# Ranks, weight differences and first-token sums in the FFN of a decoder layer: a change of order

## The chip, the cores and the metric

One core of one Trainium2 chip runs the whole kernel. The metric is the device time of one execution, in microseconds (us); smaller is better. Figures below come from three timed runs and from one execution that the hardware profiler recorded.

## What is computed

The reference is one decoder layer on x of 512 tokens by 2048, in float32: an RMSNorm, one input projection, three token mixers side by side, an output projection with residual, and then the part that the change is about:

```
x = x + concat(ya, yb, yc) @ w_out          # 2048 x 2048
h = rmsnorm(x, ffn_norm)
x = x + (silu(h @ w_gate) * (h @ w_up)) @ w_down   # 2048 x 5632, twice; 5632 x 2048
out = rmsnorm(x, final_norm)
```

## The kernel before

**Numbers in two halves.** Every float32 operand of a product is split into a high part (`hi`, rounded by ScalarE's copy, L197) and the low rest (`lo`, VectorE's subtraction, L198). A product is then three matmuls (hi by hi, hi by lo, lo by hi). `split` (L196) does this for weights and activations alike.

**Phase 1** (attention and most of the output projection, to L1096) isn't touched, but for the name of a context manager. **Phase 2** (L1106 on) does the rest: the last 512 rows of the output projection (`pp`, then `bt` token tile by token tile in `by_token_tile`, L1143), the norm of each token tile (`tail_norm`, L1182), the FFN, and the final norm.

**The FFN products.** `w_gate` and `w_up` are worked off in chunks of 256 columns: 11 blocks of 512 columns (b), four chunks each (i = 0 to 3: gate, up, gate, up), 44 chunks. A chunk is a 2 x 2 block product (weights a, b, c, d of 128 columns by 1024 rows; activations A11, A12, A22 and the sums S1 to S4) done with seven products P1 to P7 in place of eight. Each product is 16 matmuls into one of three PSUM banks, named X (P1, P4, P6, P7), Z (P5, P3) and V (P2) with g for gate and u for up: Zg is the Z bank of a gate chunk. Weights of P5, P6, P7 and P4 are differences of the loaded blocks, made on VectorE by `sub` (L1254, its instruction at L1258). In regular chunks (42 of 44), P1's block of code makes t3 = c-b and b-a, P5's makes c-(b-a) over c, P6's makes t4 = d-c; t3 and t4 live in tiles of the tag `xq` (four tiles, L1257). The first gate and the first up chunk run interleaved and make every difference in place (`weights_in_place`, L1267); they are unchanged in this.

**Beside each chunk** runs a quarter of the down product of the block before (`down`, L1366): four steps `d` with 12 matmuls each (tile `fd`), which read `w_down` and the finished activations `aT`. It loads its running sum from DRAM (Y) into two `xq` tiles, adds `fd` to it (L1385) and stores it again (L1389). `ORDER` (L1412) is the order of a chunk: P1, d, P5, d, P6, P2, d, P7, d, P4, d, P3 (the last d only stores). When the last product of a half chunk is added, `done` runs: the gate's sum and Silu (L1345, L1346), or the up's sum (L1352), the product with the gate (L1354) and the split into `aT`.

**The hand-over.** `tail_norm` forms for the token tiles 2 and 3 the sums that the seven products need: s3 (L1194), S1 (L1195), S2 (L1196), S4 (L1197). `turn` (L1205) transposes one source on TensorE, eight 128 x 128 transposes (tile `hps`), four to a bank, through three PSUM banks (`psat`), and splits them (L1219, L1220). The list at L1401 gives the order of products and turns of the first two chunks.

**Tiles that are handed round.** Six raw tiles take all weight loads (`raws`), four `ring` tiles the high halves of chunk weights and both halves of `w_down` (`rings`), four `lo` tiles the chunks' low halves; a new user waits until the last reader of the tile is done.

**What sets the order of instructions.** TensorE's order is that of the program (L116). For the other engines and the DMA queue of SyncE a planner lays down one fixed order when the program is built: with its own estimates of durations it gives each free engine, of the instructions that are ready by then, the one of lowest rank. A rank is a running count over the program. Inside `with tc.high_priority():` the count starts again at 0, and behind the block it goes on from where it stood; so the first instruction of every such block has rank 0, its tenth rank 9, wherever the block stands. Nearly all work of phase 2 on the other engines stands in such blocks: loads and splits of weights, sums, evacuations, `tail_norm`. On the chip each engine works through its fixed order.

```
raw = raws.tile([P, 1024], F32, name=f"raw{uid[0]}", tag="raw")    # six
w = rings.tile([P, 2, 512], F32R, name=f"w{uid[0]}", tag="ring")   # four
lo = fp.tile([P, 1024], F32R, name=f"lo{uid[0]}", tag="lo", bufs=4)
```

Of the kernel before, what the change touches and what calls it, by code (L numbers as in the profile page):

```python
# [31 lines left out]
F32 = mybir.dt.float32  # L32
# [75 lines left out]
def tile_hymba(ctx: ExitStack, tc: tile.TileContext, x, attn_norm, w_in, q1, k1, q2, k2, da_norm, hg_norm,  # L108
# [46 lines left out]
    uid = [0]  # L155

# [83 lines left out]
    def wstream(src, kts, col0, n, keep=None, parts=1, step=0):  # L240
# [5 lines left out]
        for g in range(0, len(kts), per_dma):  # L246
            ks = kts[g:g + per_dma]
            uid[0] += 1
            with tc.high_priority():
# [7 lines left out]
            for a in range(0, len(ks), per):  # L257
                kk = ks[a:a + per]
                uid[0] += 1
                with tc.high_priority():  # L260
# [8 lines left out]
    def proj_d(src, col0, n, act_t, evac, name, kts=range(KT), banks=None):  # L269
# [12 lines left out]
        for j in range(n // P):  # L282
            with tc.high_priority():
                evac(j, ps[j])
# [8 lines left out]
    def proj_t(src, col0, n, act_t, evac, name, kts=range(KT), banks=None, of=None, **parts):  # L293
# [12 lines left out]
        for tt in range(NT):  # L306
            with tc.high_priority():
# [12 lines left out]
    def proj_t256(src, col0, act_t, evac, name):  # L320
# [7 lines left out]
        for j in range(2):  # L328
            with tc.high_priority():
# [6 lines left out]
    with ExitStack() as p1:  # L336
# [133 lines left out]
        def b_project(th):  # L470
# [3 lines left out]
            if th == 0:  # L474
                for j in range(2):
                    with tc.high_priority():
# [629 lines left out]
    with ExitStack() as p2:  # L1106
        fp = p2.enter_context(tc.tile_pool(name="fp", bufs=1))
# [35 lines left out]
        def by_token_tile(ccs, ws, act_of, X, tail, between=None):  # L1143

            for tt in range(NT):
                c = slice(tt * P, (tt + 1) * P)
                for i, cc in enumerate(ccs):
# [6 lines left out]
                    with tc.high_priority():  # L1154
                        ev_add(cc, X, True)(tt, ps)
                with tc.high_priority():
# [25 lines left out]
        def tail_norm(tt):  # L1182
# [8 lines left out]
            if tt >= 2:  # L1191
# [4 lines left out]
                dve.tensor_tensor(h0a, h2a, h0a, op=ALU.subtract)  # L1196
                dve.tensor_tensor(h0b, h0b, h0a, op=ALU.subtract)  # L1197
# [7 lines left out]
        def turn(k, pr):  # L1205

            src = source(k, pr)
            for b in range(2):
# [5 lines left out]
                with tc.high_priority():  # L1214
# [7 lines left out]
        for cc in range(2):  # L1222
            proj_t(w_out2, cc * 512, 512, mT, ev_add(cc, X, True), f"pp{cc}", kts=range(4), banks=banks(f"pp{cc}"))
        ws = resident(w_out2, 0, (2, 3), [fp.tile([P, 4, 2, T], F32R, name=f"wo{cc}", tag="wo", bufs=2) for cc in (2, 3)])
        early = {(2, 4): ("A11", 0), (2, 6): ("A12", 0), (3, 4): ("A11", 1), (3, 6): ("A12", 1)}
        by_token_tile((2, 3), ws, lambda k: (hi_of(mT, k), lo_of(mT, k)), X, tail_norm,
                      lambda tt, n: turn(*early[tt, n]) if (tt, n) in early else None)

        wg, wu, wd = w_gate[0], w_up[0], w_down[0]
        NB = D_FF // 512  # L1230
        A["S2"], A["S3"] = wide("S2"), wide("S3")
        C = [[slots.tile([P, 2, 512], F32, name=f"C{i}{j}", tag="slot") for j in range(2)] for i in range(2)]
        aTs = [slots.tile([P, 2, T], F32R, name=f"aT{j}", tag="slot") for j in range(4)]
        A["S4"] = [slots.tile([P, 2, 2, 256], F32R, name=f"S4{j}", tag="slot") for j in range(4)]
        XF = []

        class Chunk:


            def __init__(self, w, col, name, C, done, in_place=False):  # L1240
                self.in_place = in_place
                self.w, self.col, self.name, self.C, self.done = w, col, name, C, done
                self.raw, self.bank, self.left = {}, {}, [{"P1", "P2", "P4"}, {"P3", "P5", "P6", "P7"}]
# [16 lines left out]
            def split(self, key):  # L1260
# [3 lines left out]
                split(hi, lo, self.raw.pop(key))  # L1264
# [26 lines left out]
            def weights(self, k):  # L1291
                if self.in_place:
                    return self.weights_in_place(k)
                if k == "P1":
                    self.load("a", 0, 0)
                    self.load("b", 0, 1)
                    self.load("c", 1, 1)
                    self.sub("t3", "c", "b")
                    self.sub("b", "b", "a")
                    return self.split("a")  # L1300
                if k == "P5":
                    self.sub("c", "c", "b")
                    return self.split("b")
                if k == "P6":
                    self.load("d", 1, 0)
                    self.sub("t4", "d", "c")
                    return self.split("c")
                if k == "P3":
                    self.load("c", 1, 1)
                return self.split({"P2": "d", "P7": "t3", "P4": "t4", "P3": "c"}[k])  # L1310

            def product(self, k):
                with tc.high_priority():
                    hi, lo = self.weights(k)
# [12 lines left out]
                with tc.high_priority():  # L1327
# [21 lines left out]
        def up_done(tiles):  # L1349
            def f(nh, c):  # L1350
# [4 lines left out]
                t = tiles[nh]  # L1355
                split(t[:, 0], t[:, 1], g.rearrange("p a t -> p (a t)"))
            return f

# [7 lines left out]
        def down(b, cc):  # L1366
# [3 lines left out]
            if not last:  # L1370
                with tc.high_priority():
# [5 lines left out]
            for kt, wh, wl in wstream(wd[b * 512:(b + 1) * 512, :], range(FB), cc * 512, 512):  # L1377
# [3 lines left out]
                if kt == FB - 1:  # L1381
                    with tc.high_priority():
# [113 lines left out]
```

## Time and profile before

| | |
|---|---|
| median of 3 runs | 2441.58 us (2440.13 to 2443.33) |
| the profiled execution | 2441.77 us |
| its span, first to last instruction | 2439.9 us |
| mean granted clock of TensorE | 0.995 of full |
| busy: TensorE, VectorE, ScalarE | 2373.3, 1580.6, 1025.3 us |
| the 16 DMA engines | 354.18 MB, mean 145 GB/s |

The span is what the trace covers; the execution's own time lies 1.9 us above it. PE is TensorE's matmuls, PEld its weight loads (which run beside them), DVE VectorE, ACT ScalarE, POOL GpSimd, and SPq the DMA queue of SyncE. A busy time says how long an engine worked, not whether somebody waited for it; the waits and the chain of waits say that. In a timeline, a bracket behind an instruction tells how long its engine was idle before it and what ended that.

### The profile page before, as it was taken

Reading aid. Unit: us, or ns where it says so; the run is one execution under the profiler, and the core shown is the slowest. Engines: PE = TensorE matmul, PEld = TensorE weight load, DVE = VectorE, ACT = ScalarE, POOL = GpSimd, SP = SyncE. Lnnn points to the kernel's source line nnn. Section 1 sums busy time; section 2 is a strip of 40 time slices with the busy share of each in tenths; the row PEclk is TensorE's granted clock in tenths of the full one; section 3 lists DMA queues with packets and bytes.
Section 4 is the critical chain, followed back from the end, with each engine's and each line's share of the span. In section 5 each row is a group of like instructions: output and inputs, shape, how many; then the busy total and the mean of one; then the engine's idle time right before and its main releaser. Section 6 shows DMA issues by size and latency. Waiting matters only on the chain.

```text
span 2439.9 us, 33020 instructions
## 1 busy us (share of the span) xinstructions
PE 2373.3 (97%) x12720; PEld 2018.6 (83%) x12720; DVE 1580.6 (65%) x2472; ACT 1025.3 (42%) x1800; POOL 51.0 (2%) x85
## 2 busy tenths in 40 slices
PE   9999999999999999989999999999999999999998
PEld 7898888998888778778888888888888888888887
DVE  6354556543656564787776777777777777777684
ACT  5343443442444443454444444444444443444452
POOL 2000000000000000000000000000000000000001
PEclk9999999999999999989999999999999999999999
DMA  6322222453221423435555555555555555655563
GB/s 204 96 80 70 72 80 86 131 140 87 62 61 53 147 78 104 156 113 164 182 181 182 185 186 184 183 186 186 181 184 184 182 184 186 190 190 181 174 198 138
DMA packets 355889, 354.18 MB, mean 145 GB/s; under 512 B 12882, under 2 KB 286738, under 8 KB 355732
## 3 DMA queue, kind: packets, MB, share of 16 engines
q1 hardware_dynamic: 355732, 352.07, 46.1%
q8 instruction: 100, 1.64, 0.3%
q14 instruction: 57, 0.47, 0.1%
HBM read 302.74 MB, written 49.28 MB: 144 GB/s over the span
## 4 chain that ended last, share of the span: by engine, by line
PE 77%; DVE 15%; issue 3%; ACT 2%; DMA 2%; POOL 0%; DVEq 0%; SPq 0%; ACTq 0%; POOLq 0%
PE fd L145 13%; PE Xu L145 7%; PE Xg L145 7%; PE pig L145 5%; PE po L145 5%; DVE raw L1258 4%; PE Zg L145 3%; PE Zu L145 3%; PE pq L145 3%; PE pcq L145 3%; PE pf L145 3%; PE Vg L145 2%; DVE lo L198 2%; PE Vu L145 2%; PE pak L145 2%
## 5 line engine op out<-in xcount | busy, mean ns | idle before, releaser
L197 ACT ACTIVATE w<-raw 128x512 fp32r<-128x512 f32 (+2 forms) x656 | 502.1, 772 | 907.1 <-PE fd L145 141.2
L198 DVE TENSOR_TENSOR w<-raw,w 128x512 fp32r<-128x512 f32 (+1 forms) x432 | 294.0, 681 | 345.9 <-ACT w L197 344.3
L145 PE MATMUL fd<-w,aT 128*128 128x512 f32 x1920 | 466.9, 392 | 0.0
L145 PEld LDWEIGHTS fd<-w,aT 128*128 128x128 f32 x1920 | 349.1, 188 | 74.5
L198 DVE TENSOR_TENSOR lo<-raw,w 128x1024 fp32r<-128x1024 f32 x224 | 268.5, 1221 | 83.5 <-ACT w L197 83.5
L145 PE MATMUL pig<-w,hT 128*128 128x512 f32 x576 | 138.3, 395 | 0.0
L145 PE MATMUL po<-w,mT 128*128 128x512 f32 x576 | 136.1, 393 | 0.0
L145 PE MATMUL Zg<-S,w 128*128 128x512 f32 x352 | 127.9, 399 | 0.2
L145 PE MATMUL Xg<-A,w 128*128 128x512 f32 x352 | 124.1, 392 | 1.1 <-DVE C L1333 1.1
L145 PE MATMUL Xu<-A,w 128*128 128x512 f32 x352 | 124.2, 392 | 0.8 <-DVE C L1333 0.8
L145 PE MATMUL Zu<-S,w 128*128 128x512 f32 x352 | 125.0, 392 | 0.0
L145 PEld LDWEIGHTS po<-w,mT 128*128 128x128 f32 x576 | 106.8, 188 | 21.5
L145 PEld LDWEIGHTS pig<-w,hT 128*128 128x128 f32 x576 | 106.2, 188 | 21.3
L145 PE MATMUL Xu<-S,w 128*128 128x512 f32 x352 | 123.1, 391 | 0.0
L145 PE MATMUL Xg<-S,w 128*128 128x512 f32 x352 | 122.7, 390 | 0.0
L145 PE MATMUL Zg<-S,lo 128*128 128x256 f32 x352 | 101.7, 289 | 20.3 <-DVE lo L198 20.3
L1258 DVE TENSOR_TENSOR raw<-raw,raw 128x1024 f32<-128x1024 f32 x92 | 112.3, 1221 | 5.8 <-DMA raw<-in_w_gate_dram 3.6
L145 PE MATMUL Zu<-S,lo 128*128 128x256 f32 x352 | 100.4, 285 | 10.2 <-DVE lo L198 10.2
L1385 DVE TENSOR_TENSOR xq<-xq,fd 128x512 f32<-128x512 f32 x156 | 103.2, 682 | 0.2
L145 PE MATMUL Xu<-A,lo 128*128 128x256 f32 x352 | 98.4, 280 | 0.0
L145 PE MATMUL Xg<-A,lo 128*128 128x256 f32 x352 | 98.4, 280 | 0.0
L145 PE MATMUL Xg<-S,lo 128*128 128x256 f32 x352 | 97.6, 277 | 0.0
(350 smaller groups left out, 4478.0 us busy)
## 6 DMA issues: line engine op xcount, KB each, us to landing
raw<-in_w_gate_dram SPq DMA_DIRECT2D x112, 512.0 KB, 4.4
raw<-in_w_up_dram SPq DMA_DIRECT2D x112, 512.0 KB, 4.4
raw<-in_w_down_dram SPq DMA_DIRECT2D x88, 512.0 KB, 4.2
raw<-in_w_in_dram SPq DMA_DIRECT2D x80, 512.0 KB, 3.7
xq<-y SPq DMA_DIRECT2D x78, 512.0 KB, 3.3
y<-xq SPq DMA_DIRECT2D x78, 512.0 KB, 2.6
raw<-in_w_out_dram SPq DMA_DIRECT2D x32, 512.0 KB, 3.8
raw<-in_w_in_dram SPq DMA_DIRECT2D x48, 256.0 KB, 3.0
```

Of the source, the lines that this page charges most:

```text
L145: return pe.matmul(o, l, r, start=start, stop=stop, **kw)
L197: act.activation(hi, src, AF.Copy)
L198: dve.tensor_tensor(lo, src, hi.bitcast(F32), op=ALU.subtract)
L1258: dve.tensor_tensor(self.raw[out], self.raw[a], self.raw[b], op=ALU.subtract)
L1385: dve.tensor_tensor(o, o, ps[tt], op=ALU.add)
```

## The change

It has five parts.

1. **Ranks.** From L1106 on `high_priority` is off (`hurry[0] = False`), so that all work of phase 2 has the running count as its rank. In phase 1 `rush()` is `high_priority` as before.
2. **Differences just in time, in place** (regular chunks). P5's code makes b-a over a, P6's loads c and makes c-(b-a) over a, P2's loads d and makes t4 = d-a, P7's makes c-b over c. `t3` is gone. `split(..., keep)` leaves the raw tile in use.
3. **Sums in order of need.** S2 and S4 of the first tokens (L1196, L1197) leave `tail_norm` for `later_sums`, called from the list just before P5 and P7. The list has a new order of turns: S1, S2, S3, A22, S4, each pair just before the product that reads it or one product ahead.
4. **P1 and P2 of the first two chunks are prepared** (loads, splits) before `by_token_tile` in the program, in place of behind it; `C`, `aT` and others are made after it.
5. **The split into `aT` is put off** (`later`, `do_later`) until behind P5 of the next chunk, or, in the last chunk, behind P3 and P4.

```
+    hurry = [True]
+    def rush():
+        return tc.high_priority() if hurry[0] else nullcontext()
...
-            with tc.high_priority():
+            with rush():
...
     with ExitStack() as p2:
+        hurry[0] = False
...
-                dve.tensor_tensor(h0a, h2a, h0a, op=ALU.subtract)
-                dve.tensor_tensor(h0b, h0b, h0a, op=ALU.subtract)
+        def later_sums(k):
+            for pr in range(2):
+                h0a, h0b = hns[pr]
+                if k == "S2":
+                    dve.tensor_tensor(h0a, hns[pr + 2][0], h0a, op=ALU.subtract)
+                else:
+                    dve.tensor_tensor(h0b, h0b, h0a, op=ALU.subtract)
...
-                split(hi, lo, self.raw.pop(key))
+                split(hi, lo, self.raw[key] if keep else self.raw.pop(key))
...
                 if k == "P1":
                     self.load("a", 0, 0)
                     self.load("b", 0, 1)
+                    return self.split("a", True)
+                if k == "P5":
+                    self.sub("a", "b", "a")
+                    return self.split("a", True)
+                if k == "P6":
                     self.load("c", 1, 1)
-                    self.sub("t3", "c", "b")
-                    self.sub("b", "b", "a")
-                    return self.split("a")
-                if k == "P5":
+                    self.sub("a", "c", "a")
+                    return self.split("a", True)
+                if k == "P2":
+                    self.load("d", 1, 0)
+                    self.sub("t4", "d", "a")
+                    self.raw.pop("a")
+                    return self.split("d")
+                if k == "P7":
                     self.sub("c", "c", "b")
-                    return self.split("b")
-                if k == "P6":
-                    self.load("d", 1, 0)
-                    self.sub("t4", "d", "c")
+                    self.raw.pop("b")
                     return self.split("c")
-                if k == "P3":
-                    self.load("c", 1, 1)
-                return self.split({"P2": "d", "P7": "t3", "P4": "t4", "P3": "c"}[k])
+                if k == "P4":
+                    return self.split("t4")
+                self.load("c", 1, 1)
+                return self.split("c")
...
-                split(t[:, 0], t[:, 1], g.rearrange("p a t -> p (a t)"))
+                later.append((tiles[nh][:, 0], tiles[nh][:, 1], g.rearrange("p a t -> p (a t)")))
...
+        for ch in (g, u):
+            for k in ("P1", "P2"):
+                ch.prepare(k)
...
-        for it in (g, "P1"), ("A22", 0), (g, "P2"), ("S1", 0), (u, "P1"), ("S3", 0), (u, "P2"), ("S2", 0), ("A22", 1), \
-                ("S1", 1), (g, "P5"), ("S4", 0), ("S2", 1), (u, "P5"), (g, "P6"), ("S3", 1), (u, "P6"), (g, "P7"), \
-                ("S4", 1), (u, "P7"), (g, "P4"), (u, "P4"), (g, "P3"), (u, "P3"):
+        for it in (g, "P1"), ("S1", 0), (g, "P2"), (u, "P1"), (u, "P2"), ("S1", 1), ("sum", "S2"), (g, "P5"), ("S2", 0), \
+                ("S2", 1), (u, "P5"), (g, "P6"), ("S3", 0), ("S3", 1), (u, "P6"), ("sum", "S4"), (g, "P7"), ("A22", 0), \
+                ("A22", 1), (u, "P7"), (g, "P4"), ("S4", 0), ("S4", 1), (u, "P4"), (g, "P3"), (u, "P3"):
...
+                    if k == "P5" or last and k in ("P3", "P4"):
+                        do_later()
```

## Rows read from the trace of the kernel before

**Rows 1.** The page, part 1: busy us (share of the span) and instructions of each engine.

```profile
PE 2373.3 (97%) x12720; PEld 2018.6 (83%) x12720; DVE 1580.6 (65%) x2472; ACT 1025.3 (42%) x1800; POOL 51.0 (2%) x85
```

**Rows 2.** Waits of TensorE: who waited for whom, us in total, times, longest.

```profile
PE Zg L145 <- DVE lo L198: 20.3, 19, 2.2
PE Zu L145 <- DVE lo L198: 10.2, 19, 1.6
PE hpsS L1212 <- DVE hf L1196: 7.7, 1, 7.7
...
PE hpsA L1212 <- DVE A L1220: 2.8, 2, 2.0
...
PE hpsS L1212 <- DVE S L1220: 2.0, 1, 2.0
```

**Rows 3.** Chain that ended last, over one chunk boundary: start us, us, what.

```profile
1626.34 2.79 PE Xu L145 x16
1630.38 1.22 DVE t3g L1258
...
1636.24 1.22 DVE t4g L1258
1637.46 1.15 DVE lo L198
1638.66 2.82 PE Zg L145 x15
1641.48 2.75 PE fd L145 x12
```

**Rows 4.** Timeline, SyncE then VectorE: start, us, engine, line, what [idle <- releaser].

```profile
2254.60 2.14 SPq L1389 DMA_DIRECT2D y<-xq  x2
...
2259.41 1.23 DVE L1258 TENSOR_TENSOR t3g<-raw,raw 128x1024 f32<-128x1024 f32 x1 [1.10 <-DMA y<-xq]
```

**Rows 5.** Timeline of VectorE over the same chunk boundary.

```profile
1629.78 0.69 DVE L1352 TENSOR_TENSOR C<-C 128x512 f32<-128x512 f32 x1 [1.23 <-ACT C L1330]
...
1641.39 0.69 DVE L198 TENSOR_TENSOR aT<-sg,aT 128x512 fp32r<-128x512 f32 x1
```

**Rows 6.** The page's group of low halves, and a high half on ScalarE's timeline.

```profile
L198 DVE TENSOR_TENSOR lo<-raw,w 128x1024 fp32r<-128x1024 f32 x224 | 268.5, 1221 | 83.5 <-ACT w L197 83.5
...
1637.51 1.06 ACT L197 ACTIVATE w<-raw 128x1024 fp32r<-128x1024 f32 x1 [0.47 <-ACT w L197]
```

**Rows 7.** Timeline of TensorE through the hand-over.

```profile
1025.40 0.40 PE L145 MATMUL Xg<-A,w 128*128 128x512 f32 x1
...
1028.18 1.04 PE L1212 MATMUL hpsA<-ident,hf 128*128 128x128 f32 x8
...
1047.02 1.94 PE L1212 MATMUL hpsS<-ident,hf 128*128 128x128 f32 x8 [7.68 <-DVE hf L1196]
...
1053.32 0.79 PE L145 MATMUL Zg<-S,w 128*128 128x512 f32 x1
...
1061.02 0.66 PE L1212 MATMUL hpsS<-ident,hf 128*128 128x128 f32 x4 [1.96 <-DVE S L1220]
...
1088.43 0.39 PE L145 MATMUL Xg<-A,w 128*128 128x512 f32 x1
```

**Rows 8.** Timeline of VectorE through the hand-over.

```profile
1027.99 1.22 DVE L1195 TENSOR_TENSOR hf<-hf,hf 128x1024 f32<-128x1024 f32 x1
...
1042.24 2.35 DVE L198 TENSOR_TENSOR lo<-raw,w 128x1024 fp32r<-128x1024 f32 x2
...
1045.65 2.35 DVE L1196 TENSOR_TENSOR hf<-hf,hf 128x1024 f32<-128x1024 f32 x2
```

**Rows 9.** The page, part 6, DMA issues: what, count, KB each, us to landing.

```profile
raw<-in_w_gate_dram SPq DMA_DIRECT2D x112, 512.0 KB, 4.4
```

**Rows 10.** Busy us by stretch: PE, PEld, DVE, ACT, POOL; clock, DMA share, GB/s.

```profile
1025.00:1040.00 15.00, 14.34 (x91) 12.64 (x89) 14.10 (x19) 9.05 (x15) 1.70 (x2) 1.00 0.28 84
...
1047.00:1057.00 10.00, 9.54 (x37) 7.89 (x38) 8.09 (x10) 3.58 (x6) 0.00 (x0) 0.53 0.16 46
```

More of the change, by code (lines that the diff above doesn't have):

```diff
@@ L23 @@
-from contextlib import ExitStack
+from contextlib import ExitStack, nullcontext
 import numpy as np
@@ L259, in wstream @@
                 uid[0] += 1
-                with tc.high_priority():
+                with rush():
                     if keep is None:
@@ L282, in proj_d @@
         for j in range(n // P):
-            with tc.high_priority():
+            with rush():
                 evac(j, ps[j])
@@ L306, in proj_t @@
         for tt in range(NT):
-            with tc.high_priority():
+            with rush():
                 evac(tt, ps[tt][:, :n])
@@ L328, in proj_t256 @@
         for j in range(2):
-            with tc.high_priority():
+            with rush():
                 evac(j, ps[j])
@@ L475, in b_project @@
                 for j in range(2):
-                    with tc.high_priority():
+                    with rush():
                         ev_pair(LF)(j, ps0[j])
@@ L1153, in by_token_tile @@
                             between(tt, 4 * i + kt)
[L1154 removed]
+                    with rush():
                         ev_add(cc, X, True)(tt, ps)
[L1156 removed]
+                with rush():
                     tail(tt)
@@ L1213, in turn @@
                 ts = slice(pr * P, (pr + 1) * P)
-                with tc.high_priority():
+                with rush():
                     for j in range(0, 4, 2) if isinstance(A[k], list) else (0,):
@@ L1223, in tile_hymba @@
             proj_t(w_out2, cc * 512, 512, mT, ev_add(cc, X, True), f"pp{cc}", kts=range(4), banks=banks(f"pp{cc}"))
[L1224 to L1227, printed above, removed]
         wg, wu, wd = w_gate[0], w_up[0], w_down[0]
         NB = D_FF // 512
[L1231 to L1235, printed above, removed]
         class Chunk:
@@ L1242, in __init__ @@
                 self.w, self.col, self.name, self.C, self.done = w, col, name, C, done
-                self.raw, self.bank, self.left = {}, {}, [{"P1", "P2", "P4"}, {"P3", "P5", "P6", "P7"}]
+                self.raw, self.bank, self.ready, self.left = {}, {}, {}, [{"P1", "P2", "P4"}, {"P3", "P5", "P6", "P7"}]
             def load(self, key, kh, nh):
@@ L1258, in sub, with split @@
                 dve.tensor_tensor(self.raw[out], self.raw[a], self.raw[b], op=ALU.subtract)
-            def split(self, key):
+            def split(self, key, keep=False):
                 uid[0] += 1
@@ L1326, in product @@
                 C = self.C
-                with tc.high_priority():
+                with rush():
                     if k in ("P1", "P4", "P5", "P6"):
@@ L1354, in f, with do_later @@
                 dve.tensor_tensor(g, g, h, op=ALU.mult)
-                t = tiles[nh]
-                split(t[:, 0], t[:, 1], g.rearrange("p a t -> p (a t)"))
-            return f
+                later.append((tiles[nh][:, 0], tiles[nh][:, 1], g.rearrange("p a t -> p (a t)")))
+            return f
+        later = []
+        def do_later():
+            while later:
+                split(*later.pop(0))
         def aT_of(b):
@@ L1370, in down @@
             if not last:
-                with tc.high_priority():
+                with rush():
                     xq = [fp.tile([P, 2, 512], F32, name=f"xq{b}{cc}{th}", tag="xq", bufs=4) for th in range(2)]
@@ L1381, in down @@
                 if kt == FB - 1:
-                    with tc.high_priority():
+                    with rush():
                         for tt in range(NT):
@@ L1418, in tile_hymba @@
                 next(d, None)
-                for k in LAST if (b, i) == (NB - 1, 3) else ORDER:
+                last = (b, i) == (NB - 1, 3)
+                for k in LAST if last else ORDER:
                     if k == "X":
```

27 lines of the change are left out of this document (22 added, 5 removed).

## The prediction

> **What bounds the kernel now.** I read the busy times first: TensorE works in 2373.3 of the 2439.9 us [rows 1], so an edit that adds and removes no matmul can win at most its idle 66.6 us and whatever a lowered clock cost. Second, the waits of TensorE [rows 2]. Two families of them lie in the code that changes. A product Z of a chunk (P5) waits for its low half `lo` from VectorE: 20.3 us in 19 Zg and 10.2 us in 19 Zu, together 30.5 us. At the hand-over from attention to FFN the transposes of S2 wait 7.7 us in one piece and others 2.0 us. The 2.8 us of hpsA belong to the early turns of A11 and A12, which stay.
>
> Third, the chain of waits through one chunk boundary, to see what ends last before Z [rows 3]. After the last X product of a chunk the path leaves TensorE: a weight difference t3, then the other differences, t4, the low half of P5, and only then Z, which begins at 1638.66. P5 needs one difference (b-a); its low half stands behind four. The differences can't be made earlier because t3 comes first and is written into one of four `xq` tiles, of which the `down` of the same chunk holds two until its store has landed: t3g at 2259.41 waits 1.10 us for the store y<-xq that was issued at 2254.60 [rows 4]. The sum that ends a chunk also stands first in VectorE's order and keeps it idle for 1.23 us, with all this queued behind it; the split of the finished aT follows Z's low half at 1641.39 [rows 5].
>
> **The change, part by part, against the profiled 2441.77 us** (0.2 us above the median of the three runs, 2441.58).
>
> *Differences just in time, in place.* Per regular chunk (42 of 44) there are four differences before and four after, five loads and five, seven splits and seven: nothing is saved in work, at 1.22 us a difference, 1.22 us a low half and 1.06 us a high half [rows 6]. What goes is t3: c-b is now written over c, and only t4 needs an `xq` tile, so a chunk wants three of the four. P5's b-a waits for nothing but P1's split. When is P5 ready then? Its high half gets the ring tile of the product four places before it, P4, which is the Xu that begins at 1626.34 and lasts 2.79 us [rows 3], so the tile is free at 1629.1. High half 1.06, low half 1.22: 1631.5. Suppose VectorE does first everything of this stretch that stands ahead in program order: two chunk sums, a gate product and the Z add (0.69 each), one `down` split (0.69) and b-a itself (1.22): 4.7 us, 1636.2. TensorE reaches Z at 1638.66 less its wait of 1.0, 1637.6. So the wait goes, with over 1 us to spare. What is late next is P6: c-(b-a) must follow P5's low half: 1.22 + 1.06 + 1.22 = 3.5 us after 1636.2 gives 1639.7, and P6 starts two items of 2.75 us (Z and one `fd`) [rows 3] after Z's 1637.6, at 1643.1: 3.4 us to spare. In the two regular chunks without a `down` between them P5 and P6 are neighbours, and the room shrinks to 0.6 us; there I keep a wait of 1 us. Of the 30.5 us I take 30 (ends: 24, if a fifth of the waits stays because the orders are planned ahead and not made at run time, and the whole 30.5).
>
> *Ranks in program order.* Before, nearly every FFN block counts its ranks from 0, so the first instruction of a far block ranks above the tenth of a near one. L1196 is such a late one: for the first two token tiles it could run once L1195 had ended, at 1029.2, but it runs at 1045.65, behind low halves of weights whose products stand after S2 in TensorE's order, and the S2 transposes stand for 7.7 us [rows 7, 8]. SyncE's queue gets the same ranks: the store of Y now keeps its place before the loads that come after it in the program. The next chunk's first load gets the tile that this chunk's t4 gives back before P2 runs, and its split can't begin before P7 has ended: three items (P2, one `fd`, P7), 8 us, for a load that lands in 4.4 [rows 9]; I cost it at nothing.
>
> *Hand-over.* From the first product at 1025.40 to the first of the next chunk at 1088.43 TensorE takes 63.0 us [rows 7]. Removed: the 7.7 and 2.0 us waits. With the idle piece the clock also went: 0.53 of full over 1047 to 1057 (close to the lower level, 1.2 GHz, against 2.4), and the first matmul of Zg took 0.79 us [rows 7, 10]. That is at most 10 x 0.47 = 4.7 us; some of it is evacuation, so I take 4.4. Together 14.1. Added: S1 of the first pair now comes right after P1, at 1028.18 where A22 stood [rows 7], and its sum L1195 ends at 1029.2 [rows 8]: 1.1 us. P5 of g follows S1 of the second pair directly; it waits for one high and one low copy, 1 us. Four times two turns now stand together, sixteen transposes that fill four tiles in three PSUM banks; the nearest row is the 1.96 us wait at 1061.02, also after transposes in a row [rows 7]. Ends 0 and 1.96, four times; I take 1 us each, since products stand ahead of every pair and VectorE's queue is then shorter. 14.1 - 1.1 - 1 - 4 = 8 us (ends 13 and 3). The cover is VectorE's time: it is busy 14.10 of the 15 us from 1025 [rows 10], and the two L1196 and two L1197 (2.3 us each pair) are now placed just before use; had it no room, each would show in full, 4.6 us, which the lower end holds.
>
> *Preparing P1 and P2 ahead, and aT's split after P5* move nothing that TensorE waits for: the four ring tiles allow those four splits early in both orders, and aT is first read two `down` steps after P5.
>
> Sum: 2441.8 - 30 - 8 = 2403.8, say **2404 us**; ends of the terms: 2398 and 2415.
>
> The Trainium skill, Perfetto Trace Analysis, Optimization Strategy, says that the same bubble repeating on the engine that should be saturated can mean too little memory for the next tile. By that, ranks alone would leave the 30.5 us, and only a tile given back removes them; the trace agrees as to t3's tile [rows 4].
>
> **Rivals.**
> *The boundary is only half cured.* The planner's order and the chip's times differ, VectorE still has all its low halves, and Z (or P6) waits half as long: 2441.8 - 15 - 8 = 2419. For: VectorE loses no work. Against: 1 to 3 us to spare above. 0.13.
> *The hand-over wins nothing* (S1 late, pairs of turns at 1.96 us, VectorE full): about 2411. 0.06.
> *The bubble moves to the load tiles.* The raw `a` is now held from P1 to P2 and `b` to P7, out of six tiles that `down` uses too. If a load then comes after its place by the share that Z waits now, 30 us stay: 2434. Against: the 8 us for 4.4 worked out above. 0.04. This is the Trainium skill's rule above turned on the new code.
> *Slower: the serial chain through `a`.* Place: P6. If P5's low half still ends only when Z starts, and the queue that VectorE now has behind it, from its end at 1638.6 [rows 3] to that of the aT split at 1642.1 [rows 5], stands before c-a, P6's low half comes 3.5 + 3.5 = 7.0 us later, against 5.5 us of cover: 1.5 us in 42 chunks, 63 us, against 38 removed: 2467. It decides from 0.9 us per chunk on. For: the three steps can no longer overlap. Against: program order ranks c-a ahead of that queue. 0.06.
> *It doesn't do what it says:* the planner finds nearly the old orders since readiness, not rank, rules; 2440. 0.04.
> The forecast keeps 0.67.
>
> **The numbers.** The forecast's own ends, 2398 to 2415, hold also the hand-over rival; the range goes on to the half-cured case, some 6 us beyond it for a hand-over that wins little, and 2 us below: 2396 to 2425, which leaves out about 0.15. A measurement here can tell 0.2%, 4.9 us, from no change. Faster: forecast and first three rivals, 0.90; same 0.04; slower 0.06.
>
> **What would show it.** Right: the waits of Zg and Zu on `lo` under 4 us together; no t3 and no y<-xq in the chain; chunks following each other every 30.4 us (eleven items of 2.76); hpsS never waiting over 2 us and a granted clock of 1.00 from 1047 to 1057; first chunk after the hand-over near 1080. Wrong: a new row of TensorE waits for X products (P6) on `lo`, or of `lo` on loads, with 19 or more entries, or the hand-over still 63 us long.

## The result and the profile after

The changed kernel takes **2406.1 us** (median of four runs, 2403.6 to 2406.7) where the kernel before takes 2440.9: a ratio of 0.9855, 95% interval 0.9838 to 0.9872. The execution that the profiler recorded is the shortest of the four, 2403.6 us with a span of 2401.8. So the change is faster by 1.5%, and the total is nearly the 2404 that was forecast. The sizes of the two terms of the forecast are both wrong, though, and by about the same amount in opposite directions, as the rows below show.

The busy times first, page part 1, to be set beside [rows 1]; the second line is part 4 of the page, the shares of the chain that ended last, by engine.

```profile
PE 2361.2 (98%) x12720; PEld 2019.1 (84%) x12720; DVE 1584.2 (66%) x2472; ACT 1032.5 (43%) x1800; POOL 50.3 (2%) x85
...
PE 94%; DVE 3%; ACT 1%; DMA 1%; issue 1%; POOL 0%; SPq 0%; ACTq 0%; POOLq 0%; DVEq 0%
```

As many matmuls as before, and VectorE has no less to do. The chain is TensorE's for 94%; the same line of the kernel before gave TensorE 77% and VectorE 15%. The waits of TensorE answer to [rows 2]:

```profile
PE hpsA L1225 <- DVE A L1233: 7.8, 3, 3.2
PE hpsS L1225 <- DVE S L1233: 6.1, 3, 3.8
...
PE Zg L145 <- DVE S L1233: 1.7, 1, 1.7
```

No Zg and no Zu waits for `lo` any more (20.3 and 10.2 us before). In their place hpsA went from 2.8 to 7.8 us (6.3 of it at the early turns, 1.6 at A22) and the waits of hpsS for split copies from 2.0 to 6.1 us; the 7.7 us behind L1196 is gone. These are the two stages of the prediction, to be read one by one.

**The chunks.** The chain of waits over one boundary, to be read against [rows 3]:

```profile
1619.52 2.77 PE Xg L145 x16
1622.29 2.77 PE fd L145 x12
1625.06 2.77 PE Zg L145 x16
```

TensorE passes from item to item, with nothing of VectorE between. VectorE's timeline of the same boundary shows why ([rows 5] before):

```profile
1616.10 1.22 DVE L1260 TENSOR_TENSOR raw<-raw,raw 128x1024 f32<-128x1024 f32 x1
1617.42 0.69 DVE L1365 TENSOR_TENSOR C<-C 128x512 f32<-128x512 f32 x1
1618.14 0.69 DVE L1367 TENSOR_TENSOR sg<-sg,C 128x512 f32<-128x512 f32 x1
1618.75 1.22 DVE L203 TENSOR_TENSOR lo<-raw,w 128x1024 fp32r<-128x1024 f32 x1
...
1622.90 1.22 DVE L1260 TENSOR_TENSOR raw<-raw,raw 128x1024 f32<-128x1024 f32 x1
```

The one difference that P5 needs is made ahead of the chunk's sums; its low half ends near 1620, 5 us before Zg.

**The hand-over.** TensorE's timeline, to be set beside [rows 7]: early transposes, first product, the longer waits between (one of 0.59 us at 1050.85 is left out), first product of the next chunk.

```profile
1017.85 0.66 PE L1225 MATMUL hpsA<-ident,hf 128*128 128x128 f32 x4 [3.18 <-DVE A L1233]
...
1028.42 0.66 PE L1225 MATMUL hpsA<-ident,hf 128*128 128x128 f32 x4 [3.09 <-DVE A L1233]
...
1029.61 0.56 PE L145 MATMUL Xg<-A,w 128*128 128x512 f32 x1
...
1045.90 0.50 PE L145 MATMUL Zg<-S,w 128*128 128x512 f32 x1 [1.70 <-DVE S L1233]
...
1060.02 0.66 PE L1225 MATMUL hpsS<-ident,s 128*128 128x128 f32 x4 [1.68 <-DVE S L1233]
...
1069.04 0.66 PE L1225 MATMUL hpsA<-ident,hf 128*128 128x128 f32 x4 [1.58 <-DVE A L1233]
...
1080.33 0.63 PE L1225 MATMUL hpsS<-ident,hf 128*128 128x128 f32 x4 [3.81 <-DVE S L1233]
...
1090.81 0.40 PE L145 MATMUL Xg<-A,w 128*128 128x512 f32 x1
```

The first product starts at 1029.61, 4.2 us later than before; the stage then takes 61.2 us in place of 63.0, and the next chunk starts 2.4 us later than before (1090.81 against 1088.43). From there to the end of the span it is 2401.8 - 1090.8 = 1311.0 us, against 2439.9 - 1088.4 = 1351.5: **40.5 us** saved in the chunks, 2.4 us lost ahead of them, 38.1 us in the spans. The medians of the two kernels differ by less, 34.7 us, since the profiled execution of the changed kernel was its shortest; so each part of the split can be off by a few us.

This split of a run (first product, length of the hand-over, rest) is how all runs below are read. Every time in the table but the median is of the profiled execution.

| kernel | first product | hand-over | rest | median | ratio to before (95%) |
|---|---|---|---|---|---|
| before | 1025.4 | 63.0 | 1351.5 | 2440.9 | 1 |
| changed | 1029.6 | 61.2 | 1311.0 | 2406.1 | 0.9855 (0.9838 to 0.9872) |
| in place alone | 1023.2 | 63.2 | 1313.9 | 2405.2 | 0.9861 (0.9847 to 0.9874) |
| ranks alone | 1029.2 | 58.9 | 1323.0 | 2414.2 | 0.9900 (0.9886 to 0.9913) |
| xq tile held | 1025.2 | 62.9 | 1312.4 | 2402.0 | 0.9847 (0.9833 to 0.9860) |
| t3 kept | 1025.4 | 62.5 | 1310.2 | 2399.4 | 0.9836 (0.9823 to 0.9850) |
| old order, no tile | 1026.8 | 62.7 | 1312.6 | 2403.2 | 0.9852 (0.9836 to 0.9869) |
| changed, aT at once | 1028.0 | 61.9 | 1310.9 | 2403.9 | 0.9858 (0.9845 to 0.9872) |
| changed, old list | 1030.0 | 59.3 | 1312.5 | 2400.7 | 0.9846 (0.9833 to 0.9860) |
| changed, copies first | 1024.7 | 61.7 | 1311.2 | 2402.0 | 0.9846 (0.9833 to 0.9860) |
| old list, copies first, table ahead (4 B) | 1026.2 | 56.9 | 1320.2 | 2406.7 | 0.9864 (0.9851 to 0.9878) |
| the same, no new tile | 1027.5 | 56.7 | 1311.4 | 2397.6 | 0.9830 (0.9815 to 0.9845) |
| the same, tile of 64 B | 1028.1 | 57.0 | 1319.6 | 2406.5 (one run) | |
| old list, copies first | 1028.1 | 56.7 | 1311.9 | **2396.4** | **0.9817** (0.9804 to 0.9831) |

Starts of the first product scatter by 3.6 us between kernels that are alike up to there: "in place alone" lies at 1023.2, before, "tile held" and "t3 kept" at 1025.2 to 1025.4, "old order, no tile" at 1026.8. So a start by itself proves little; below it is counted from the first matmul of `bt`.

### The profile page after: what moved, and what is told of

Its sections match the earlier page's. It is cut to its first block, busy times and chain, and to the rows that moved or that the text cites. A ratio compares the mean times of both kernels' runs of the same rounds, so it can differ in the third digit from the quotient of the medians.

```text
span 2401.8 us, 32892 instructions
## 1 busy us (share of the span) xinstructions
PE 2361.2 (98%) x12720; PEld 2019.1 (84%) x12720; DVE 1584.2 (66%) x2472; ACT 1032.5 (43%) x1800; POOL 50.3 (2%) x85
## 4 chain that ended last, share of the span: by engine, by line
PE 94%; DVE 3%; ACT 1%; DMA 1%; issue 1%; POOL 0%; SPq 0%; ACTq 0%; POOLq 0%; DVEq 0%
PE fd L145 18%; PE Xu L145 10%; PE Xg L145 10%; PE pig L145 6%; PE po L145 5%; PE Zg L145 5%; PE Zu L145 5%; PE pq L145 3%; PE pf L145 3%; PE pcq L145 3%; PE Vg L145 2%; PE Vu L145 2%; PE bt L145 2%; PE pak L145 2%; PE pk L145 2%; PE sc L145 2%
## 5 line engine op out<-in xcount | busy, mean ns | idle before, releaser
L202 ACT ACTIVATE w<-raw 128x512 fp32r<-128x512 f32 (+2 forms) x698 | 549.0, 790 | 926.7 <-PE fd L145 148.4
L203 DVE TENSOR_TENSOR lo<-raw,w 128x1024 fp32r<-128x1024 f32 x266 | 323.3, 1223 | 179.0 <-ACT w L202 179.0
L1260 DVE TENSOR_TENSOR raw<-raw,raw 128x1024 f32<-128x1024 f32 x134 | 163.4, 1219 | 6.8 <-DMA raw<-in_w_gate_dram 3.2
```

The costliest lines, as they stand in the source:

```text
L202: act.activation(hi, src, AF.Copy)
L203: dve.tensor_tensor(lo, src, hi.bitcast(F32), op=ALU.subtract)
L1260: dve.tensor_tensor(self.raw[out], self.raw[a], self.raw[b], op=ALU.subtract)
```

## The experiments

**One part at a time.** The in-place differences alone, in the kernel before:

```
 if k == "P1":
     self.load("a", 0, 0)
     self.load("b", 0, 1)
-    self.load("c", 1, 1)
-    self.sub("t3", "c", "b")
-    self.sub("b", "b", "a")
-    return self.split("a")
+    return self.split("a", True)
...
```

> The kernel before with the in-place differences alone: t3 gone, b-a made at P5, c-(b-a) at P6, all high priorities, the hand-over list and the immediate split of aT as before. Theory (the tile that t3 held, and its wait for the store of Y, make the boundary wait): the waits of Zg and Zu on lo, 30.5 us together before, fall under 4 us, the chunks follow each other every 30.4 us, and the time from the next chunk's first product to the end falls from 1351.5 us to about 1311, as in the changed kernel; the hand-over stays at 63 us with its 7.7 us wait; total 2400 to 2405. Rival (program order gives the boundary gain): the Zg and Zu waits stay above 20 us and the total stays within 5 us of 2441. Second rival (both are needed): between, near 2420.

Measured: 2405.2 us, no wait of Zg or Zu on `lo` in the list, and 1313.9 us from the next chunk's first product on. The hand-over stays as it was, with its long wait of 7.9 us behind L1196.

This part by itself gives what the whole change gives (0.9861 and 0.9855, intervals nearly the same). The ranks alone:

```
     with ExitStack() as p2:
+        hurry[0] = False
...
-                with tc.high_priority():
+                with rush():
...
```

> The kernel before with the program-order ranks alone in the FFN; t3, its xq tile, the hand-over list and the immediate split of aT as before. Theory (the tile makes the wait): Zg and Zu still wait 20 us or more on lo, t3 still stands in the chain behind the store of Y, and from the next chunk's first product to the end it takes 1340 us or more; the total is 2430 to 2446, where the hand-over decides by a few us. Rival (program order gives the gain): the Zg and Zu waits fall under 4 us and the total is 2400 to 2410.

Measured: 2414.2 us, 1323.0 us of chunks, and neither theory right. The tile theory wanted 20 us of Z waits, the rival under 4. Of 30.5 us in 38 waits, 8.6 us in 19 are left, and none at Zu:

```profile
PE Zg L145 <- DVE lo L203: 8.6, 19, 1.0
```

VectorE's timeline before one Zg (which starts at 1627.18) shows t3 still first after the sum, and what the ranks did move: t4, which stood ahead of P5's low half [rows 3], now stands behind it.

```profile
1619.50 1.22 DVE L1264 TENSOR_TENSOR t3g<-raw,raw 128x1024 f32<-128x1024 f32 x1
...
1625.91 1.22 DVE L203 TENSOR_TENSOR lo<-raw,w 128x1024 fp32r<-128x1024 f32 x1
...
1628.29 1.22 DVE L1264 TENSOR_TENSOR t4g<-raw,raw 128x1024 f32<-128x1024 f32 x1
```

So either part works on the boundary: the ranks win some 28 of 40 us (1351.5 to 1323.0), the differences nearly all. The two gains don't add.

**What in the old differences made the wait?** The prediction's chain has two links: t3 takes an xq tile that `down` gives back late, and b-a, written over b, must follow t3. First, the tile is kept busy and nothing else:

```
+    b = self.load("b", 0, 1)
+    self.held = fp.tile([P, 1024], F32, name=f"t3{self.name}", tag="xq", bufs=4)
+    dve.tensor_tensor(self.held[:, :1], b[:, :1], b[:, :1], op=ALU.subtract)
     return self.split("a", True)
...
```

> The in-place differences alone (as in the run before, 2405 us), but each chunk takes an xq tile at P1 and holds it to P7, as t3's was held; one column is written into it and read from it, no t3 is made. Theory A (my step: t3's tile, free only when the store of Y has landed, makes the boundary wait): the Zg and Zu waits on lo come back with 20 us or more, the total is 2425 to 2441. Theory B (VectorE's work ahead of P5's low half makes it, the tile does not): waits under 4 us, 2403 to 2408.

Measured: 2402.0 us, no Z wait on `lo`. The one-column write comes late, as t3 did, but nobody needs it; P5's difference is made ten microseconds earlier:

```profile
1612.70 1.22 DVE L1258 TENSOR_TENSOR raw<-raw,raw 128x1024 f32<-128x1024 f32 x1
...
1622.63 0.15 DVE L1298 TENSOR_TENSOR t3g<-raw 128x1 f32<-128x1 f32 x1
```

A tile that is held doesn't by itself make the bubble. Next, t3 itself is kept, in its tile, with the other differences made in `a`:

```
     self.load("b", 0, 1)
+    self.load("c", 1, 1)
+    self.sub("t3", "c", "b")
     return self.split("a", True)
...
```

> The in-place differences with t3 = c-b made first again, at P1 in an xq tile, with c loaded there; b-a and c-(b-a) are made in place in a, so b-a does not read what t3 writes. All high priorities as before. Four differences per chunk as in all kernels. Theory B (what counts is how much VectorE has to do between the end of the last chunk and P5's low half; t3's 1.22 us stands first again): about half to all of the wait of before comes back, Zg and Zu wait 10 to 30 us together, total 2415 to 2441. Theory A (t3's tile and its wait for the store): the same waits. Theory C (that b-a had to wait for t3 through b): waits under 4 us, total 2403 to 2408.

Measured: 2399.4 us, no Z wait on `lo`: theory C. In program order t3 stands first; on VectorE it now starts 7 us after P5's low half does:

```profile
1610.90 1.22 DVE L1258 TENSOR_TENSOR raw<-raw,raw 128x1024 f32<-128x1024 f32 x1
...
1614.41 1.22 DVE L198 TENSOR_TENSOR lo<-raw,w 128x1024 fp32r<-128x1024 f32 x1 [0.50 <-ACT w L197]
...
1621.43 1.22 DVE L1258 TENSOR_TENSOR t3g<-raw,raw 128x1024 f32<-128x1024 f32 x1
```

Then the opposite: the old order c-b, then b-a over b, but no xq tile for c-b.

```
     self.load("c", 1, 1)
-    self.sub("t3", "c", "b")
+    self.sub("c", "c", "b")
     self.sub("b", "b", "a")
...
 if k == "P6":
+    self.sub("a", "c", "a", ALU.add)
...
```

> The kernel before with its order of differences kept (c-b first, then b-a over b, so that b-a must follow c-b), but c-b written over c, in no xq tile; c-(b-a) is then formed as (c-b)+a. High priorities, hand-over list and aT's split as before. Theory D (both halves of the old chain are needed: the tile that t3 waits for, and b-a that must follow t3): without the tile c-b can be made as soon as c has landed, the Zg and Zu waits fall under 4 us, total 2399 to 2406. Theory E (the link alone does it: with two differences ahead of P5's low half VectorE is late, tile or not): Zg and Zu wait 15 us or more together, total 2420 to 2441.

Measured: 2403.2 us, no Z wait on `lo`: theory D. Both differences stand far ahead of the boundary (Zg of this chunk starts at 1623.62):

```profile
1599.66 1.23 DVE L1258 TENSOR_TENSOR raw<-raw,raw 128x1024 f32<-128x1024 f32 x1 [2.34 <-DMA raw<-in_w_gate_dram]
1600.81 1.22 DVE L198 TENSOR_TENSOR lo<-raw,w 128x1024 fp32r<-128x1024 f32 x1
1601.94 1.22 DVE L1258 TENSOR_TENSOR raw<-raw,raw 128x1024 f32<-128x1024 f32 x1
```

The three runs together: the tile without the link costs nothing, t3 with its tile but without the link costs nothing, the link without the tile costs nothing. Under the old high priorities only both together, as in the kernel before, hold P5 back. One rival is argued away and not tested. All three runs also write c-(b-a) and t4 one product later, and on VectorE both then stand behind P5's low half in the first two, t4 in the third. But in each that low half ends 6.0 to 6.1 us before its Zg (1617.44 against 1623.46, 1615.63 against 1621.67, 1617.55 against 1623.62), and the two differences take 2.4 us. No run moved them alone. That most of the waits went with the ranks, which left t3 first and put t4 behind, suggests that the length of this queue counts too.

**The later split of aT.** Undone in the changed kernel:

```
-                later.append((tiles[nh][:, 0], tiles[nh][:, 1], g.rearrange("p a t -> p (a t)")))
+                split(tiles[nh][:, 0], tiles[nh][:, 1], g.rearrange("p a t -> p (a t)"))
```

> The changed kernel with the split of aT made at once with the product of gate and up, in place of after P5's product. Theory (nothing waits for it; program order puts the next chunk's P5 low half behind it, but there is over 1 us to spare): the same time as the changed kernel, 2404 to 2408, Zg and Zu waits on lo under 4 us. Rival (the late split is what lets P5's low half through in time): each of the 22 Zg boundaries loses up to the 0.7 to 1.2 us of one or two of the split's instructions, 15 to 26 us in all, 2421 to 2432.

Measured: 2403.9 us and 1310.9 us of chunks against 1311.0. It costs and gives nothing, as predicted.

**The hand-over.** The old list and the old place of the sums, in the changed kernel:

```
                 dve.tensor_tensor(h2a, h2a, h2b, op=ALU.add)
+                dve.tensor_tensor(h0a, h2a, h0a, op=ALU.subtract)
+                dve.tensor_tensor(h0b, h0b, h0a, op=ALU.subtract)
...
-        for it in (g, "P1"), ("S1", 0), (g, "P2"), (u, "P1"), (u, "P2"), ("S1", 1), ("sum", "S2"), (g, "P5"), ("S2", 0), \
+        for it in (g, "P1"), ("A22", 0), (g, "P2"), ("S1", 0), (u, "P1"), ("S3", 0), (u, "P2"), ("S2", 0), ("A22", 1), \
...
```

> The changed kernel with the old list of the hand-over (single turns between the products) and all sums of the first tokens made at once in the norm of the last token tile. Theory (the new list costs: four pairs of turns wait 7.66 us in the changed kernel, the old single turns 2.0 and one long wait): with program-order ranks the sums no longer come late, so the 7.7 us wait of the S2 transposes goes as well and the hand-over, first product to the next chunk's first, falls from 61.2 to 55 to 58 us; total 2400 to 2403. Rival (the old list loses with these ranks too: the sums L1196 and L1197 now stand in VectorE's order ahead of the early turns' copies and the first products' splits): the early transposes wait some 4 us more than in the changed kernel, the total is 2408 to 2416.

Measured: 2400.7 us, hand-over 59.3 us. The long wait for L1196 stays away, so the ranks removed it and not the list; that 59.3 is more than the 55 to 58 expected comes from two waits for copies:

```profile
1043.90 0.92 PE L1227 MATMUL hpsS<-ident,s 128*128 128x128 f32 x4 [2.81 <-DVE S L1235]
...
1060.66 0.63 PE L1227 MATMUL hpsS<-ident,hf 128*128 128x128 f32 x4 [2.47 <-DVE S L1235]
```

Next, the copies of all turns at high priority, with the new list:

```
                 ts = slice(pr * P, (pr + 1) * P)
-                with rush():
+                with tc.high_priority():
```

> The changed kernel with the copies of all turns (both engines) at high priority again, all else ranked in program order. Theory (behind program-order ranks the early turns' copies stand behind the norm and the sums of the last token tile): the waits of the early transposes fall from 7.8 us to 3 us, the first product starts 3 to 5 us earlier, at 1025 to 1027, and the last double turn loses the 1.2 us of a difference ahead of it; total 3 to 6 us less than the changed kernel, 2400 to 2403 where the kernel before takes 2440.9. Rival (the copies then push the sums and splits of P1 and P2 back, which wait in their place): within 1.5 us of the changed kernel.

Measured: 2402.0 us; the first product starts at 1024.71. The early transposes now wait 1.53 and 0.54 us where they waited 3.18 and 3.09:

```profile
1015.50 0.66 PE L1225 MATMUL hpsA<-ident,hf 128*128 128x128 f32 x4 [1.53 <-DVE A L1233]
1023.52 0.66 PE L1225 MATMUL hpsA<-ident,hf 128*128 128x128 f32 x4 [0.54 <-DVE A L1233]
```

The profiled spans differ by 4.2 us and the medians by 4.1, both within what was expected, but the two were not timed side by side, and the intervals of their ratios overlap. Nor does the start hold by itself: three of the four later kernels with the copies first start at 1027.5 to 1028.1. What shows the copies' rank to be a cause is the way from the first matmul of `bt` to the first product. Its starts in the kernel before and in the changed one:

```profile
996.52 14.68 PE L145 MATMUL bt<-wo,mT 128*128 128x512 f32 x63 [0.69 <-issue]
```

```profile
997.30 14.68 PE L145 MATMUL bt<-wo,mT 128*128 128x512 f32 x63 [1.28 <-issue]
```

That way takes 28.9 us before and 29.0 to 29.4 in the other four kernels with the old priorities. It takes 32.3 us in the changed kernel and 32.6 to 32.8 in the other three with the copies in program order (ranks alone, aT at once, old list). With the copies first it takes 28.1 here and 28.8 to 30.6 in the four kernels that follow.

**Both, and Silu's table.** In the changed kernel ScalarE loads a table for Silu (1.28 us at 1077.23) between copies that the last double turn waits for. A one-element Silu ahead takes the load out of the stage:

```
         s4 = fp.tile([P, NT, 4], F32, name="s4")
+        warm = fp.tile([P, 1], F32, name="warm")
+        act.activation(warm, mhalf[:, :1], AF.Silu)
...
-                with rush():
+                with tc.high_priority():
...
```

> The changed kernel with the old hand-over list and all sums in the norm (2400.7 us by itself), the copies of all turns at high priority, and Silu's table loaded once ahead, by a one-element Silu at the start of the FFN. Theory (the old list's hand-over of 59.3 us stays, the first product starts 4 us earlier and a table load of 1.28 us leaves the path): 2395 to 2398, or 0.980 to 0.983 of the kernel before. Rival (with the copies first, the sums for S1 and S2 come late again, as before the change): the transposes of S wait 4 us or more in one piece and the total is 2400 or above.

Measured: a hand-over of 56.9 us, better than any before, and still 2406.7 us: the rest takes 1320.2 us, 9 more than elsewhere, with no wait that the others don't have. The products themselves are slower (section on the unexpected, below). So the same without the new tile, and with a wide one:

```
-        warm = fp.tile([P, 1], F32, name="warm")
-        act.activation(warm, mhalf[:, :1], AF.Silu)
+        act.activation(s4[:, 0, :1], mhalf[:, :1], AF.Silu)
```

> As the run with the old list, the turns' copies first and Silu's table loaded ahead, which took 2406.7 us; the one-element Silu now writes into a tile that is there anyway, in place of a new tile of 4 bytes per partition. Theory (the new tile moved the tiles allocated behind it by 4 bytes, and products then took 2.80 to 2.81 us each in place of 2.74 to 2.77, some 9 us from the hand-over to the end): products take 2.77 us again, the first product starts at 1026, the next chunk at 1083, and from there to the end it takes 1311 us: total 2394 to 2397. Rival (the slower products come from the early copies or the table): 2403 to 2408.

> The same with the one-element Silu writing into a new tile of 64 bytes per partition. Theory (what costs is an offset of 4 bytes, not a new tile): products take 2.77 us, total 2394 to 2398. Rival (any shift of these tiles costs): products take 2.80 us or more, total 2403 to 2408.

Measured: without a tile 2397.6 us and 1311.4 us of chunks; with a tile of 64 bytes (one run) 2406.5 and 1319.6. The theory of an offset of 4 bytes falls, and its rival, that any new tile in this place costs, holds. Last, without the Silu ahead (the line above taken out):

> The changed kernel with the old hand-over list, all sums in the norm and the turns' copies first, but without the one-element Silu ahead (with it 2397.6 us, hand-over 56.7 us from the first product at 1027.5 to the next chunk's first at 1084.2). Theory (the 1.28 us table load of Silu stands on the path at the end of the hand-over): the hand-over is 57.5 to 58.5 us, the total 1 to 2 us more, 2398.5 to 2400. Rival (the load is hidden behind products, as it was before the change, and the gain is the list and the copies alone): hand-over 56.7 us, total 2396.5 to 2398.5.

Measured: 2396.4 us, hand-over 56.7 us as with it: the rival. ScalarE's timeline has the load still in the stage, where no wait of TensorE lies beside it (in the old list no turn stands there; what the load costs in the new list, no run tells):

```profile
1078.14 1.28 ACT L1361 ACT_TABLE_LOAD   x1
```

This last kernel is the fastest of the study, 0.9817 of the kernel before (0.9804 to 0.9831), and its interval lies below the changed kernel's. It is the changed kernel with the copies of the turns first and the third part of the change taken back. The longest wait left in its hand-over is 2.96 us at 1050.91, P5 of g for its low half, which stands on VectorE behind copies that now go first, a sum (L1203) and a chunk sum.

## Why the prediction came out right

**The boundary wait goes: right, and so is the chain given for it.** t3 in its xq tile, b-a behind it, the low half behind both: in the three runs above neither link makes a wait without the other, with the open end named there. One thing was put too strongly. The trace had t3 wait for the store only twice in all chunks, 1.10 us [rows 4] and once more:

```profile
DVE t3u L1258 <- DMA y<-xq: 1.0, 1, 1.0
```

The rows of "tile held" and "old order, no tile" suggest that the tile acts through the fixed order of VectorE, which puts what is written into it after the chunk's sums, and not through a wait that a row shows.

**Its size: mis-sized, 30 us for 40.5.** The term was the sum of the waits in the list. A gate chunk and an up chunk together took 62.79 us in the kernel before (from the first matmul of one Zg to that of the next, 1597.82 to 1660.61) and 60.80 after (1586.19 to 1646.99): 1.99 us won, while the two waits in that stretch are 1.01 and 0.48 us. TensorE's timeline of the kernel before shows where the rest hides:

```profile
1637.26 0.39 PE L145 MATMUL Zg<-S,w 128*128 128x512 f32 x1
1638.66 0.39 PE L145 MATMUL Zg<-S,lo 128*128 128x256 f32 x1 [1.01 <-DVE lo L198]
1638.88 0.40 PE L145 MATMUL Zg<-S,w 128*128 128x512 f32 x1
1639.12 0.28 PE L145 MATMUL Zg<-S,lo 128*128 128x256 f32 x1
1639.24 0.39 PE L145 MATMUL Zg<-S,w 128*128 128x512 f32 x1
```

The wait is counted from the end of the first high matmul, 0.39 us after its start. Without a wait the next one starts 0.24 us after it (1638.88, then 1639.12). So 0.15 us is lost while TensorE counts as busy, and the matmul that waited has its successor 0.22 us on where others have it after 0.12, another 0.10. That is about 0.25 us for each of 38 listed waits, 9.5 us, nearly all of the 10 that were missing; it fits that TensorE's busy time fell by 12.1 us with the same matmuls ([rows 1] and the line above), though a part of that is the clock at the hand-over. The run with ranks alone goes the same way: 8.6 us listed in 19 waits, 12.0 us over the changed kernel's rest, 0.18 more for each.

**The fallback "ranks alone would leave the 30.5 us": wrong.** The prediction leaned there on the Trainium skill, Perfetto Trace Analysis, Optimization Strategy, which says that a repeating bubble can mean too little memory for the next tile. Read as the only cause, it fails here twice: the ranks alone, with the tile still taken, left 8.6 us of waits, and with the tile held but nothing behind it there were none. A tile given back does cure the bubble, as the run with the old order and no tile shows; it is one way out, not the only one, and the measurement decides.

**The cover of P6 and of the loads: right.** No X product waits for `lo` or a load in the stretch of the chunks; VectorE makes c-(b-a) at 1622.90, and none of the rivals of that kind (serial chain through `a`, bubble at the raw tiles, half cure) came.

**The hand-over: wrong, -8 us forecast, +2.4 measured.** The stage itself, from first product to the next chunk's, won 1.8 us of the 8, and the first product came 4.2 us late, which the forecast had at nothing. Three steps failed.

First, the 2.8 us of hpsA "belong to the early turns, which stay". They stay in the program, but their copies lost their rank. VectorE's timeline ahead of the first product:

```profile
1022.41 2.48 DVE L1194 SCALAR_TENSOR_TENSOR hf<-x,rs,gain 128x1024 f32<-128x1024 f32 x2 [0.95 <-POOL rs L199]
1024.81 1.22 DVE L1200 TENSOR_TENSOR s<-hf,hf 128x1024 f32<-128x1024 f32 x1
1025.95 0.68 DVE L1135 TENSOR_TENSOR x<-x,bt 128x512 f32<-128x512 f32 x1
1026.55 1.22 DVE L1201 TENSOR_TENSOR hf<-hf,hf 128x1024 f32<-128x1024 f32 x1
1027.68 1.88 DVE L1233 TENSOR_TENSOR A<-hpsA,A 128x512 fp32r<-128x512 f32 x3
```

The norm, the sums and a residual addition rank ahead, and the copies L1233 for which hpsA waits come only after 5.3 us of them. The two early waits grew from 2.02 + 0.81 to 3.18 + 3.09 us, 3.4 of the 4.2 us by which the first product is late; the other 0.8 us lies ahead of `bt` already (997.30 against 996.52). With the copies first the two waited 1.53 + 0.54 us. The prediction followed every wait that the ranks would remove and didn't ask which of the old high priorities had been protecting something.

Second, the four double turns, put at 4 us between ends of 0 and 7.8, took 0.59 + 1.68 + 1.58 + 3.81 = 7.66 us, the upper end. The S4 wait of 3.81 has Silu with its table (1.28 us, at 1077.23) on ScalarE and a weight difference on VectorE between the copies:

```profile
1077.97 0.75 DVE L1233 TENSOR_TENSOR S<-hpsS,S 128x256 fp32r<-128x256 f32 x2
1078.63 1.22 DVE L1260 TENSOR_TENSOR raw<-raw,raw 128x1024 f32<-128x1024 f32 x1
1079.76 2.07 DVE L1233 TENSOR_TENSOR S<-hpsS,S 128x256 fp32r<-128x256 f32 x5
```

With the waits at P5 (1.70; 1 us was forecast) the stage has 9.4 us of waits against 7.68 + 0.36 + 1.96 = 10.0 before: the 9.7 us that were removed came back almost in full. The 1.1 us put down for S1 of the first pair didn't show: its sum (1026.55 above) is made while TensorE waits for the first product; with the copies first it does wait, 0.90 us.

Third, the clock. It is 1.00 from 1047 to 1057, as forecast, but the loss moved to the places where TensorE idles now (columns as in [rows 10], clock third from last):

```profile
1025.00:1040.00 15.00, 11.91 (x65) 10.30 (x63) 14.09 (x17) 6.22 (x11) 1.71 (x2) 0.89 0.10 36
1047.00:1057.00 10.00, 9.41 (x62) 8.32 (x61) 8.93 (x10) 5.28 (x9) 0.00 (x0) 1.00 0.53 149
1065.00:1100.00 35.00, 29.61 (x173) 25.79 (x172) 25.35 (x36) 17.81 (x29) 0.00 (x0) 0.95 0.24 69
```

At most 15 x 0.11 + 35 x 0.05 = 3.4 us; the first matmuls after the idle piece take 0.63 us in place of 0.40. Of the 4.4 us counted as regained about 1 was left. The stage adds up: waits of 9.4 and at most 3.4 for the clock make 12.8 us, against 10.0 and at most 4.7 before, 1.9 less, and it became 1.8 us shorter.

So the total fits because the chunks won 10.5 us more and the hand-over 10.4 us less than forecast. That the two cancel is luck; the mechanism at the boundary, which is most of the gain, was foreseen. Of the signs named beforehand, those of the chunks came (no wait of Z on `lo`, 30.4 us a chunk); hpsS never waiting over 2 us and a next chunk near 1080 did not. The rival "the hand-over wins nothing" (2411 with the old term for the chunks) was right in its own part.

**The new list.** That order of need costs rather than gives was not among the cases. With ranks in program order the old list's stage takes 59.3 us against 61.2; with the copies first 56.7 against 61.7. The pairs of turns in a row are what the old list avoids. With the copies first the four pairs still wait 0.59 + 0.96 + 1.59 + 3.00 = 6.1 us, so the copies' rank explains only 1.5 of the 7.66. The next chunk, forecast near 1080, started at 1090.8, and in the fastest kernel of the study at 1084.8. That the pairs are the reason is argued from these waits; no run took only one pair apart, and the old list always came with the old place of the sums.

## What to carry to other kernels

Where a wait repeats, look for the whole chain behind the late operand, memory and data dependences together: cutting either link was enough here, and a bubble that looks like a missing tile went away while the tile stayed taken. Size such a wait by the period of the repeating stretch with and without it, not by the list of waits, which missed a quarter here. Before a blanket high priority is taken away, list what each use of it protects, and keep the few that feed TensorE's next transpose.

## What had not been expected of the hardware

A tile of 4 or of 64 bytes per partition, allocated at the start of the FFN and used once, made the chunks 8 to 9 us slower, with no wait in them and a granted clock of 1.00 in both. Matmuls begun in 300 us, with the tile of 64 bytes and, second fence, without a new tile (the columns are those of [rows 10]):

```profile
1500.00:1800.00 300.00, 300.00 (x1570) 256.35 (x1569) 218.51 (x253) 129.35 (x166) 0.00 (x0) 1.00 0.59 192
```

```profile
1500.00:1800.00 300.00, 300.00 (x1580) 257.58 (x1580) 220.60 (x257) 130.22 (x168) 0.00 (x0) 1.00 0.58 190
```

In the chains of waits of the two, from 1575 to 1650, a product takes 2.80 to 2.82 us and a step of `fd` 2.73 to 2.76 with the tile, and 2.74 to 2.78 for both kinds without it. The slowness starts before the chunks: 63 matmuls of `bt` take 14.95 and 14.88 us with the new tile (4 and 64 bytes) and 14.67 or 14.68 in all other kernels here. Since TensorE's instructions are the same, the place of the tiles allocated behind it is the likely cause. Products read `lo` and `bt` reads `wo`, which lie in the pool that got the new tile, while the operands of `fd` lie in others; so these two are the likely ones. That is argued, not tested, and which boundary in memory counts, no run here tells. The effect is as large as the gain that was being measured, so an experiment that adds a tile, however small, should look at the time of one matmul first.
